# Three 256-column matmuls into one region in place of a 512- and a 256-column matmul with a join, in the weight-stationary products of a two-layer decoder trunk

## The chip, the cores and the metric

The kernel runs on one core of a Trainium2 chip. The core has a matrix engine (TensorE; PE in the profile, with its weight loads shown as a row of their own, PEld), a vector engine (VectorE, DVE), an activation engine (ScalarE, ACT), a general engine (GpSimd, POOL) and an engine that issues transfers (SyncE, SP). They run side by side and wait for one another by semaphores. Working data lies in on-chip memory of 128 partitions; the matrix engine adds its results up in a separate accumulation memory, which is divided into banks. A bank holds 512 float32 columns here.

The metric is the device time of one execution in microseconds (us), as the median of several runs.

## The reference

One sequence of 256 positions with 2048 features goes through two layers. Each layer mixes positions by attention, then applies an MLP; after each there is a residual sum and a layer norm:

```python
x = layer_norm(ALPHA * x + mixed, ln1_g[layer], ln1_b[layer])
x = layer_norm(ALPHA * x + sqrelu_mlp(x, mlp_w1[layer], mlp_w2[layer]), ...)

def sqrelu_mlp(x, w1, w2):
    hid = jax.nn.relu(jnp.einsum('bsd,df->bsf', x, w1))     # 2048 -> 8192
    return jnp.einsum('bsf,fd->bsd', hid * hid, w2)         # 8192 -> 2048
```

Layer 0 mixes with sliding-window attention (16 query heads, 2 key heads) and with three dilated window patterns of 8 heads, all from one input projection of 2048 to 5888 features. Layer 1 mixes with 16 heads of stick-breaking attention and 16 heads of latent attention, whose queries and keys come from small latent vectors. Everything is float32, and the weights are some 395 MB that are read once.

## The kernel before

**Arithmetic.** Every large product is made of three. An operand is split into a high part, rounded to the matrix engine's float32r format, and a low part, the difference. A product is hi x hi + hi x lo + lo x hi. Weights are split by the class `Stream`: units of 128 x 1024 weights come by DMA (line 95, up to 5 units ahead), are rounded on ScalarE (line 128, `w_hi`) and subtracted on VectorE (line 129, `w_lo`), up to 3 units ahead. Activations are kept feature-major in k-tiles of 128 features x 512 columns: columns 0 to 255 hold the high part of the 256 positions, columns 256 to 511 the low part (`parts`, line 300).

**Two kinds of product.** `as_` (line 348) holds activations stationary and streams weights: three matmuls per k-tile and token tile (lines 379 to 381), 512 columns wide as a rule and 256 or 288 in a few projections. It gives a token-major result. `ws` (line 312) holds weights stationary and streams activations, and gives a feature-major result. It is used for the query and key projections of layer 0 and of the stick-breaking heads, and for the first matrix of both MLPs. `uq` (line 927) does the same for the latent queries. These two are what the change touches. `ukv` (line 960) makes latent keys and values and isn't touched; its keys are weight-stationary and made by three matmuls of 256 columns each (lines 970 to 972).

**A product in `ws`.** Let the weights of 128 features and one k-tile be `wh`, `wl`, the activations `xh`, `xl`. Line 333 loads `wh` and streams both halves of the k-tile, 512 columns: the first half of the bank sums `wh` x `xh`, the second half `wh` x `xl`. Line 334 loads `wl` and streams `xh`, 256 columns, into the second half. After all 16 k-tiles the bank holds two sums, which `join` (line 341) adds: ScalarE copies the second half out of the bank, scaled (line 345, tile `xfull`), and VectorE adds the first half to it (line 346). In the MLP the ReLU is then a separate ScalarE instruction on 512 columns (line 1073), followed by the square and its split (lines 1074 to 1076). These three steps are put off to a later unit through the queue `late`.

**Loops and order.** `ws` takes the weights unit by unit. A unit of a 512-wide block holds two k-tiles of four feature tiles. For each feature tile the unit's k-tiles follow each other, so 8 products run without a break. After each unit `pump` (line 196) puts in one step of other work: a put-off step, a step of side work and a step of attention. The order of instructions on each engine is that of the program text; nothing is reordered by a scheduler.

**Banks.** There are four kinds of tiles in the accumulation memory: `acc` (4 banks), `sc` (2), `pt` (1) and `o` (1). Before, a 512-wide block of `ws` takes four banks. In the MLP every second block takes `sc`, `sc`, `pt` and `o` in place of the four `acc` (line 318), so that one block can be joined while the next is summed.

Of the kernel before, what the change touches and what calls it, by code (L numbers as in the profile page):

```python
# [67 lines left out]
class Stream:  # L68
    """Weights in the order of their use: DMA ahead, split ahead into two float32r parts.
    For the next shared units GpSimd takes a share of the second part."""  # L70
# [73 lines left out]
class LazyTiles:  # L144
    """feature-major k-tiles that are made when a product comes near them"""
# [13 lines left out]
class Job:  # L159
    """one group of attention heads: scores, then stages of the weighting, then the values"""  # L160
# [11 lines left out]
class Trunk:  # L172
# [22 lines left out]
    # ---- work beside the products: one step per unit of weights  # L195
# [17 lines left out]
    def queue(self, job, u=None):  # L213
        """all heads; pattern u only, when the patterns come one by one"""
        if u is None:
            self.todo.extend((job, h, 0) for h in range(job.n))
        else:
            self.todo.extend((job, h, u) for h in range(job.n))
# [42 lines left out]
    def flip(self, job, h, u):  # L261
        """weights of a head (and pattern) to keys-major"""
        nc = self.nc
        st = job.s[h]
        pt = self.ps.tile([P, 384], F32, name="pt")
        for b in range(3):
            nc.tensor.transpose(pt[:, b * P:(b + 1) * P], st[:, u * 384 + b * P:u * 384 + (b + 1) * P], self.ident)
        pT = self.at.tile([P, 384], F32, name="pT", bufs=self.pt_bufs)
        nc.scalar.copy(pT, pt)
        job.pt[(h, u)] = pT  # L270
        if u == job.per - 1 and (job.per > 1 or h % 2):
            self.s_live -= 1
# [30 lines left out]
    # ---- psum  # L303
# [3 lines left out]
    # ---- matrix products; xs: per k-tile (hi, lo) of [128, 256]  # L307
# [4 lines left out]
    def ws(self, xs, nkt, width, take, more=False):  # L312
        """weights stationary, feature-major result. Per 128 features one bank: the first 256 columns sum
        hi x hi, the other 256 the two cross terms; take(f, bank) is called when the sums of tile f are complete"""
        nc = self.nc
        nf = width // P
        if more:
            banks = [self.ps.tile([P, 512], F32, name=n, bufs=m) for n, m in (("sc", 2), ("sc", 2), ("pt", 1), ("o", 1))]
        else:
            banks = [self.acc() for _ in range(nf)]  # L320
        kt = 0
        while kt < nkt:
            self.near(xs, kt, 1024 // width, nkt)
            end = kt + 1024 // width >= nkt
            hi, lo, n, wd = self.w.next(ahead=self.split_ahead - end)
            assert wd == width
            self.near(xs, kt + 2, 1024 // width, nkt)
            for f in range(nf):
                for kk in range(n):
                    xh, xl, both = xs[kt + kk]  # L330
                    c = kk * width + f * P
                    first, last = kt + kk == 0, kt + kk == nkt - 1
                    nc.tensor.matmul(banks[f], hi[:, c:c + P], both, start=first, stop=False, skip_group_check=True)  # L333
                    nc.tensor.matmul(banks[f][:, S:2 * S], lo[:, c:c + P], xh, start=False, stop=last, skip_group_check=True)  # L334
                if kt + n == nkt:
                    take(f, banks[f])
            kt += n
            if kt < nkt:
                self.pump()

    def join(self, out, bank, scale=1.0):
        """both sums of a bank, scaled by a power of two"""
        nc = self.nc
        t = self.small.tile([P, S], F32, name="xfull", bufs=3)
        nc.scalar.activation(t, bank[:, S:2 * S], AF.Copy, scale=scale)  # L345
        nc.vector.scalar_tensor_tensor(out, bank[:, 0:S], scale, t, op0=ALU.mult, op1=ALU.add)

    def as_(self, xs, nkt, width, hold=0):
        """activations stationary: token-major result [128 tokens, width] for both token tiles;
        the last hold units of weights serve first the one token tile, then the other"""  # L350
# [35 lines left out]
    # ---- weights in the order in which the products below take them  # L386
# [58 lines left out]
    # ---- set-up  # L445
# [52 lines left out]
    def transposed(self, ln, z=None):  # L498
        """x (token-major) to feature-major k-tiles, split; ln=(which, layer) applies its gain and bias"""
# [28 lines left out]
    def keep_clock(self, n, t=None):  # L528
        """products that nothing takes, while the array waits, so that its clock is not halved"""
        t = self.ident if t is None else t  # L530
        o = self.ps.tile([P, 512], F32, name="pt")
        for _ in range(n):
            self.nc.tensor.matmul(o[:, 0:t.shape[1]], t[:, 0:P], t, start=True, stop=True, skip_group_check=True)

    # ---- residual sums and layer norm
# [17 lines left out]
    def rstd(self, var, n, eps, scale=1.0):  # L553
        """(var * scale + eps) ** -0.5"""
        nc = self.nc
        ve = self.small.tile([P, 2], F32, name="ve")
        nc.vector.tensor_scalar(ve[:, :n], var, scale, eps, op0=ALU.mult, op1=ALU.add)  # L557
        r = self.small.tile([P, 2], F32, name="rs")
        nc.gpsimd.tensor_tensor(r[:, :n], ve[:, :n], self.mhalf[:, :n], op=ALU.pow)  # L559
        return r  # L560

    def moments(self, last, stats):
        """the last column block into x, and per token tile the mean and 1/deviation"""
        nc = self.nc
        outs, c, first = last
        res = []
        for t in range(2):
            self.add_one(outs[t], t, c, first, stats)
            mv = self.small.tile([P, 2], F32, name="mv")
            nc.vector.bn_aggr(mv, stats[t])  # L570
            res.append((mv, self.rstd(mv[:, 1:2], 1, LN_EPS)))
            yield res[t]
# [17 lines left out]
    def x_new(self, ln, layer):  # L590
        """the residual's copy of the normed x, token-major"""
# [36 lines left out]
    def final(self, last, stats):  # L628
        """the last layer norm, token-major, to the output"""
# [33 lines left out]
    # ---- attention  # L663
    def qk(self, sc, q, k):
        """q, k: feature-major [K, 256]; sc: q-block 0 in 128 columns, q-block 1 in 256"""
# [4 lines left out]
    def softmax(self, per, scale=1.0, sink=None):  # L670
        """three stages: maximum, exponentials, division"""
# [43 lines left out]
    # ---- layer 0 mixer  # L715
    def even(self):
# [8 lines left out]
        def take(f, bank):  # L725
            self.join(kvf[:, f, :], bank)
            if f == 0:
                for kv in range(2):
                    for half in range(2):
                        eng = nc.scalar.copy if half else nc.vector.tensor_copy  # L730
                        eng(kd[half * HD:half * HD + HD, kv, :], kvf[kv * HD:kv * HD + HD, 0, :])
# [81 lines left out]
    def project(self, width, tag="qk", scale=1.0):  # L813
        """feature-major projection of x; tiles of [128, 2, 256] with two heads to a slice"""
        out = [self.tile2(tag) for _ in range(width // 256)]
        self.ws(self.xT, KT, width, lambda f, bank: self.join(out[f // 2][:, f % 2, :], bank, scale))
# [3 lines left out]
    # ---- layer 1 mixer  # L820
# [106 lines left out]
    def uq(self):  # L927
        """queries of 4 latent heads, rotated; per tile 2 heads, features in rows 0-95"""
        nc = self.nc
        banks = [self.acc() for _ in range(4)]  # L930
# [11 lines left out]
        for u in range(2):  # L942
            hi, lo, n, wd = self.w.next(ahead=self.split_ahead - u)
            for h in range(4):
                for kk in range(n):
                    xh, xl, both = self.lq[kt + kk]
                    c = (kk * 4 + h) * P
                    k = kt + kk
                    nc.tensor.matmul(banks[h], hi[:, c:c + P], both, start=k == 0, stop=False, skip_group_check=True)
                    nc.tensor.matmul(banks[h][:, S:2 * S], lo[:, c:c + P], xh, start=False, stop=k == 3, skip_group_check=True)  # L950
                if u:
                    q = qs[h // 2]
                    self.join(q[:, h % 2, :], banks[h])
                    if h % 2:
                        self.late.append(lambda q=q: rotate(q))
# [4 lines left out]
    def ukv(self):  # L960
        """keys (rows 0-63 from the latents, 64-95 the shared rotated ones) and values of 8 latent heads"""
# [91 lines left out]
    # ---- MLP  # L1053
    def mlp(self, layer):
        nc = self.nc
        st = self.new_stats()
        for q in range(4):
            hs = []
            cur = {}

            def take(f, bank):
                if f % 2 == 0:
                    cur["r"] = self.mp.tile([P, 512], F32, name="relu", bufs=3)
                r = cur["r"]
                self.join(r[:, (f % 2) * S:(f % 2) * S + S], bank)
                if f % 2 == 0:
                    return
                sq = self.mp.tile([P, 512], F32, name="sq", bufs=2)
                hh = self.mp.tile([P, 512], F32R, name="h_hi", bufs=12)
                hl = self.mp.tile([P, 512], F32R, name="h_lo", bufs=12)  # L1070

                def square():
                    nc.scalar.activation(r, r, AF.Relu)
# [8 lines left out]
            for b in range(4):  # L1082
                self.ws(self.xT, KT, 512, take, more=b % 2 == 1)
# [64 lines left out]
```

## Time and profile before

| | |
|---|---|
| time, median of 3 runs | 2272.68 us (2270.44 to 2273.03) |
| span of the profiled execution | 2269.1 us |
| TensorE matmul | 2228.8 us busy, 98%, 11633 instructions |
| TensorE weight load | 1857.5 us busy, 82%, 11633 instructions |
| VectorE | 1435.0 us busy, 63% |
| ScalarE | 1064.9 us busy, 47% |
| DMA | 399.09 MB, mean 176 GB/s |
| mean granted TensorE clock | 0.993 |

The profiled execution has its own span, 2269.1 us, from its first to its last instruction; the median of the timed runs is 3.6 us above it. Durations in the profile belong to that one execution.

Two things help to read the rows. A matmul's duration runs from its start to the end of its results, and the next one starts long before that end. So the pace of the matrix engine is not the duration of its instructions, but the distance from one start to the next. And a group's mean is of one form of instruction; the names in "out<-in" are those of the program's tiles, where `x` is a k-tile of the layer's input, `y` one of the latents or of the attention outputs, `w_hi` and `w_lo` are split weights, and `acc`, `sc`, `pt` and `o` are banks.

### The profile page before, as it was taken

The page shows a single profiled execution, that of the slowest core. Times are in us where ns is not written, and L with a number is a line of the kernel's source. Part 1 is how long each engine was busy: PE and PEld are TensorE (multiplying, and loading weights), DVE is VectorE, ACT ScalarE, POOL GpSimd, SP SyncE. Part 2 cuts the span into 40 slices and gives each one's busy share as a digit, 9 for nine tenths or more (in the row PEclk, how much of TensorE's full clock was granted, in tenths as well). Part 3 has the DMA queues.
Part 4 walks back from the last instruction along what each step waited for, and adds up shares of the span by engine and source line. Part 5 has one row for each costly group of instructions (what it writes and reads, how often), then busy time and mean ns, then how long its engine had stood idle before and what let it go on. Part 6 is the DMA issues. An engine that isn't in the chain of part 4 may idle for free. (4 is left out here: it accounts for less than half of the span.)

```text
span 2269.1 us, 30281 instructions
## 1 busy us (share of the span) xinstructions
PE 2228.8 (98%) x11633; PEld 1857.5 (82%) x11633; DVE 1435.0 (63%) x1967; ACT 1064.9 (47%) x1573; POOL 132.4 (6%) x125
## 2 busy tenths in 40 slices
PE   8999999999999999999999999999999999999997
PEld 7878787788888888888878878777888888888885
DVE  6766455785455556556567797978655655554655
ACT  4554344355345345345444575735534534443542
POOL 3000000120000000000024101003000000000001
PEclk9999999999999999999999999999999999999998
DMA  7445454465656665665658544355666566656553
GB/s 248 140 121 150 130 166 142 139 209 191 193 178 195 194 187 181 198 187 177 202 144 223 160 135 135 128 170 177 233 193 193 175 207 180 194 193 187 186 193 104
DMA packets 224322, 399.09 MB, mean 176 GB/s; under 512 B 12778, under 2 KB 56512, under 8 KB 223408
## 3 DMA queue, kind: packets, MB, share of 16 engines
q1 hardware_dynamic: 221760, 387.30, 54.6%
q0 software_dynamic: 2416, 9.84, 1.6%
q8 instruction: 91, 1.49, 0.3%
q14 instruction: 55, 0.45, 0.1%
HBM read 395.00 MB, written 2.10 MB: 175 GB/s over the span
## 5 line engine op out<-in xcount | busy, mean ns | idle before, releaser
L129 DVE TENSOR_TENSOR w_lo<-raw,w_hi 128x1024 fp32r<-128x1024 f32 (+3 forms) x748 | 879.0, 1188 | 589.9 <-ACT w_hi L128 583.0
L128 ACT CAST w_hi<-raw 128x1024 fp32r<-128x1024 f32 (+2 forms) x788 | 763.0, 986 | 777.2 <-PE acc L381 453.6
L333 PE MATMUL acc<-x,w_hi 128*128 128x512 f32 x1824 | 661.0, 405 | 12.4 <-DVE x L520 11.6
L334 PE MATMUL acc<-x,w_lo 128*128 128x256 f32 x1824 | 514.5, 282 | 0.0
L333 PEld LDWEIGHTS acc<-x,w_hi 128*128 128x128 f32 x1824 | 345.9, 190 | 106.7 <-DVE x L520 14.8
L381 PE MATMUL acc<-w_hi,h_lo 128*128 128x512 f32 x1016 | 399.3, 393 | 0.0
L380 PE MATMUL acc<-w_lo,h_hi 128*128 128x512 f32 x1016 | 398.0, 392 | 0.0
L379 PE MATMUL acc<-w_hi,h_hi 128*128 128x512 f32 x1016 | 395.6, 389 | 0.0
L334 PEld LDWEIGHTS acc<-x,w_lo 128*128 128x128 f32 x1824 | 348.0, 191 | 1.1 <-POOL w_lo L129 0.5
L380 PEld LDWEIGHTS acc<-w_lo,h_hi 128*128 128x128 f32 x1016 | 190.8, 188 | 43.2
L379 PEld LDWEIGHTS acc<-w_hi,h_hi 128*128 128x128 f32 x1016 | 190.7, 188 | 42.4
L381 PEld LDWEIGHTS acc<-w_hi,h_lo 128*128 128x128 f32 x1016 | 190.9, 188 | 39.5
L333 PE MATMUL sc<-x,w_hi 128*128 128x512 f32 x512 | 186.1, 397 | 0.0
L334 PE MATMUL sc<-x,w_lo 128*128 128x256 f32 x512 | 143.6, 281 | 0.0
L379 PE MATMUL acc<-w_hi,x 128*128 128x256 f32 (+2 forms) x400 | 137.3, 343 | 3.9 <-DVE x L519 3.8
L380 PE MATMUL acc<-w_lo,x 128*128 128x256 f32 (+2 forms) x400 | 133.4, 333 | 0.1
L381 PE MATMUL acc<-w_hi,x 128*128 128x256 f32 (+2 forms) x400 | 133.3, 333 | 0.0
L333 PEld LDWEIGHTS sc<-x,w_hi 128*128 128x128 f32 x512 | 96.1, 188 | 23.5
L559 POOL TENSOR_TENSOR rs<-ve,mhalf 128x1 f32<-128x1 f32 (+1 forms) x10 | 6.6, 659 | 1849.8 <-DVE ve L557 1843.8
L345 ACT ACTIVATE xfull<-acc 128x256 f32<-128x256 f32 x130 | 49.8, 384 | 127.0 <-PE acc L334 107.7
L334 PEld LDWEIGHTS sc<-x,w_lo 128*128 128x128 f32 x512 | 96.7, 189 | 0.0
L333 PE MATMUL o<-x,w_hi 128*128 128x512 f32 x256 | 96.0, 397 | 0.0
(194 smaller groups left out, 2376.1 us busy)
## 6 DMA issues: line engine op xcount, KB each, us to landing
raw<-in_mlp_w SPq DMA_DIRECT2D x512, 512.0 KB, 4.1
raw<-in_even_w_in SPq DMA_DIRECT2D x92, 512.0 KB, 4.0
raw<-in_odd_w_in SPq DMA_DIRECT2D x56, 512.0 KB, 4.4
raw<-in_odd_w_out SPq DMA_DIRECT2D x32, 512.0 KB, 3.7
raw<-in_even_w_out SPq DMA_DIRECT2D x24, 512.0 KB, 3.7
gb_rows<-in_ln_g POOLq DMA_DIRECT2D x3, 1024.0 KB, 6.7
gb_rows<-in_ln_b POOLq DMA_DIRECT2D x3, 1024.0 KB, 8.6
raw<-in_odd_w_uq SPq DMA_DIRECT2D x8, 384.0 KB, 3.6
```

What stands on the lines that cost most here:

```text
L128: nc.scalar.copy(h, r)
L129: (nc.gpsimd if i and perm is None else nc.vector).tensor_tensor(l, r, h.bitcast(F32), op=ALU.subtract)
L333: nc.tensor.matmul(banks[f], hi[:, c:c + P], both, start=first, stop=False, skip_group_check=True)
L334: nc.tensor.matmul(banks[f][:, S:2 * S], lo[:, c:c + P], xh, start=False, stop=last, skip_group_check=True)
L345: nc.scalar.activation(t, bank[:, S:2 * S], AF.Copy, scale=scale)
L379: nc.tensor.matmul(outs[t], xh[:, ts], hi[:, c:c + width], start=first, stop=False, skip_group_check=True)
L380: nc.tensor.matmul(outs[t], xh[:, ts], lo[:, c:c + width], start=False, stop=False, skip_group_check=True)
L381: nc.tensor.matmul(outs[t], xl[:, ts], hi[:, c:c + width], start=False, stop=last, skip_group_check=True)
L559: nc.gpsimd.tensor_tensor(r[:, :n], ve[:, :n], self.mhalf[:, :n], op=ALU.pow)
```

## The change

`ws` and `uq` no longer stream both halves of a k-tile at once. A product is three matmuls of 256 columns that add up in the same 256 columns of a bank: `wh` x `xh`, `wh` x `xl`, `wl` x `xh`, each with its own stationary operand in the program. Two feature tiles share a bank, one in each half. `join` is gone: when both feature tiles of a bank are complete, ScalarE takes the whole bank of 512 columns out at once, with the scale for projections and the ReLU for the MLP. A 512-wide block takes two `acc` banks, and the MLP no longer takes `sc`, `pt` and `o`. Comments and docstrings are removed as well.

```diff
-    def ws(self, xs, nkt, width, take, more=False):
-        nf = width // P
-        if more:
-            banks = [self.ps.tile([P, 512], F32, name=n, bufs=m) for n, m in (("sc", 2), ("sc", 2), ("pt", 1), ("o", 1))]
-        else:
-            banks = [self.acc() for _ in range(nf)]
+    def ws(self, xs, nkt, width, take):
+        banks = [self.acc() for _ in range(width // 256)]
...
-            for f in range(nf):
+            for f in range(width // P):
+                o = banks[f // 2][:, (f % 2) * S:(f % 2) * S + S]
                 for kk in range(n):
-                    xh, xl, both = xs[kt + kk]
+                    xh, xl, _ = xs[kt + kk]
                     c = kk * width + f * P
-                    first, last = kt + kk == 0, kt + kk == nkt - 1
-                    nc.tensor.matmul(banks[f], hi[:, c:c + P], both, start=first, stop=False, skip_group_check=True)
-                    nc.tensor.matmul(banks[f][:, S:2 * S], lo[:, c:c + P], xh, start=False, stop=last, skip_group_check=True)
-                if kt + n == nkt:
-                    take(f, banks[f])
+                    self.three(o, hi[:, c:c + P], lo[:, c:c + P], xh, xl, kt + kk == 0 and f % 2 == 0, kt + kk == nkt - 1)
+                if kt + n == nkt and f % 2:
+                    take(f // 2, banks[f // 2])
...
-    def join(self, out, bank, scale=1.0):
-        t = self.small.tile([P, S], F32, name="xfull", bufs=3)
-        nc.scalar.activation(t, bank[:, S:2 * S], AF.Copy, scale=scale)
-        nc.vector.scalar_tensor_tensor(out, bank[:, 0:S], scale, t, op0=ALU.mult, op1=ALU.add)
+    def three(self, o, wh, wl, xh, xl, first, last):
+        mm = self.nc.tensor.matmul
+        mm(o, wh, xh, start=first, stop=False, skip_group_check=True)
+        mm(o, wh, xl, start=False, stop=False, skip_group_check=True)
+        mm(o, wl, xh, start=False, stop=last, skip_group_check=True)
...
-        self.ws(self.xT, KT, width, lambda f, bank: self.join(out[f // 2][:, f % 2, :], bank, scale))
+        self.ws(self.xT, KT, width, lambda p, bank: self.nc.scalar.activation(
+            out[p].rearrange("p a s -> p (a s)"), bank, AF.Copy, scale=scale))
...
-                self.join(r[:, (f % 2) * S:(f % 2) * S + S], bank)
-                if f % 2 == 0:
-                    return
+            def take(p, bank):
+                r = self.mp.tile([P, 512], F32, name="relu", bufs=3)
+                nc.scalar.activation(r, bank, AF.Relu)
...
                 def square():
-                    nc.scalar.activation(r, r, AF.Relu)
                     nc.scalar.activation(hh, r, AF.Square)
...
-                self.ws(self.xT, KT, 512, take, more=b % 2 == 1)
+                self.ws(self.xT, KT, 512, take)
```

`uq` and the take-out of the shared keys in layer 0 are changed in the same way.

More of the change, by code (lines that the diff above doesn't have):

```diff
@@ L310, in near @@
             xs.need(min(kt + n - 1, nkt - 1))
-    def ws(self, xs, nkt, width, take, more=False):
-        nc = self.nc
-        nf = width // P
-        if more:
-            banks = [self.ps.tile([P, 512], F32, name=n, bufs=m) for n, m in (("sc", 2), ("sc", 2), ("pt", 1), ("o", 1))]
-        else:
-            banks = [self.acc() for _ in range(nf)]
+    def ws(self, xs, nkt, width, take):
+        banks = [self.acc() for _ in range(width // 256)]
         kt = 0
@@ L339, in ws @@
                 self.pump()
-    def join(self, out, bank, scale=1.0):
-        nc = self.nc
-        t = self.small.tile([P, S], F32, name="xfull", bufs=3)
-        nc.scalar.activation(t, bank[:, S:2 * S], AF.Copy, scale=scale)
-        nc.vector.scalar_tensor_tensor(out, bank[:, 0:S], scale, t, op0=ALU.mult, op1=ALU.add)
+    def three(self, o, wh, wl, xh, xl, first, last):
[3 more added lines that the diff above has]
+        mm(o, wl, xh, start=False, stop=last, skip_group_check=True)
     def as_(self, xs, nkt, width, hold=0):
@@ L723, in even @@
         vf = kvf[:, 1, :]
[L725 to L731, printed above, removed]
+        def take(p, bank):
+            nc.scalar.copy(kvf.rearrange("p a s -> p (a s)"), bank)
+            for kv in range(2):
+                for half in range(2):
+                    eng = nc.scalar.copy if half else nc.vector.tensor_copy
+                    eng(kd[half * HD:half * HD + HD, kv, :], kvf[kv * HD:kv * HD + HD, 0, :])
         self.ws(self.xT, KT, 256, take)
@@ L929, in uq @@
         nc = self.nc
-        banks = [self.acc() for _ in range(4)]
+        banks = [self.acc() for _ in range(2)]
         qs = [self.tile2("d") for _ in range(2)]
@@ L944, in uq @@
             for h in range(4):
+                o = banks[h // 2][:, (h % 2) * S:(h % 2) * S + S]
                 for kk in range(n):
-                    xh, xl, both = self.lq[kt + kk]
+                    xh, xl, _ = self.lq[kt + kk]
                     c = (kk * 4 + h) * P
[L948 to L951, printed above, removed]
+                    self.three(o, hi[:, c:c + P], lo[:, c:c + P], xh, xl, kt + kk == 0 and h % 2 == 0, kt + kk == 3)
+                if u and h % 2:
                     q = qs[h // 2]
-                    self.join(q[:, h % 2, :], banks[h])
-                    if h % 2:
-                        self.late.append(lambda q=q: rotate(q))
+                    nc.scalar.copy(q.rearrange("p a s -> p (a s)"), banks[h // 2])
+                    self.late.append(lambda q=q: rotate(q))
             kt += n
@@ L1058, in mlp, with take @@
             hs = []
-            cur = {}
-            def take(f, bank):
-                if f % 2 == 0:
-                    cur["r"] = self.mp.tile([P, 512], F32, name="relu", bufs=3)
-                r = cur["r"]
-                self.join(r[:, (f % 2) * S:(f % 2) * S + S], bank)
-                if f % 2 == 0:
-                    return
+            def take(p, bank):
+                r = self.mp.tile([P, 512], F32, name="relu", bufs=3)
                 sq = self.mp.tile([P, 512], F32, name="sq", bufs=2)
```

## The prediction, made before the result

> **What bounds the kernel now.** I read the page first, then the waits of the matrix engine, its groups by shape, and its timeline.
>
> ```profile
> span 2269.1 us, 30281 instructions
> PE 2228.8 (98%) x11633; PEld 1857.5 (82%) x11633; DVE 1435.0 (63%) x1967; ACT 1064.9 (47%) x1573; POOL 132.4 (6%) x125
> PEclk9999999999999999999999999999999999999998
> ```
>
> The matrix engine is busy for 98% of the span at a granted clock of 0.9 or more of full speed in all but the last slice. Busy is not the same as "at its best", because records of pipelined matmuls overlap; so I ask next what it waits for, and then how far apart its matmuls start.
>
> ```profile
> PE acc L333 <- DVE x L520: 11.6, 9, 3.6
> PE acc L379 <- DVE x L519: 3.8, 1, 3.8
> PE sc L667 <- DVE S L1026: 2.4, 5, 1.1
> PE acc L333 <- ACT w_hi L128: 0.4, 2, 0.2
> ```
>
> The columns are the total in us, the number of times and the longest. The large waits are those for the split x tiles after a layer norm (lines 519 and 520), which the change doesn't touch. Split weights cost 0.4 us in all, and no line says that a matmul waits for a bank that a join has still to empty. So the time is the sum of start-to-start distances on the matrix engine, and the change must be priced there.
>
> ```profile
> L333 PE MATMUL acc<-x,w_hi 128*128 128x512 f32 x1824 | 661.0, 405 | 12.4 <-DVE x L520 11.6 <-ACT w_hi L128 0.4
> L333 PE MATMUL sc<-x,w_hi 128*128 128x512 f32 x512 | 186.1, 397 | 0.0
> L333 PE MATMUL o<-x,w_hi 128*128 128x512 f32 x256 | 96.0, 397 | 0.0
> L333 PE MATMUL pt<-x,w_hi 128*128 128x512 f32 x256 | 95.9, 397 | 0.0
> L949 PE MATMUL acc<-y,w_hi 128*128 128x512 f32 x64 | 23.4, 405 | 0.0
> L379 PE MATMUL acc<-w_hi,x 128*128 128x256 f32 x192 | 56.4, 294 | 0.0
> L970 PE MATMUL acc<-y,w_hi 128*128 128x256 f32 x16 | 4.8, 302 | 0.0
> ```
>
> The first five rows give the number of products that are changed: 1824 + 512 + 256 + 256 + 64 = 2912 (a product is one block of 128x128 weights against one k-tile). The last two rows are places where the kernel before already does three 256-column matmuls per product.
>
> **The change on the matrix engine.** Now a product is one matmul of 512 columns and one of 256, each with its own weight load. Afterwards it is three of 256, each with its own load: the streamed columns stay at 768, one load and one start are added. The pace of the pair, from the timeline (columns: start, duration, engine, line), in the MLP of layer 0 and then in that of layer 1:
>
> ```profile
> 879.61 0.40 PE L333 MATMUL sc<-x,w_hi 128*128 128x512 f32 x1
> 879.85 0.28 PE L334 MATMUL sc<-x,w_lo 128*128 128x256 f32 x1
> ...
> 895.87 0.39 PE L379 MATMUL acc<-w_hi,h_hi 128*128 128x512 f32 x1
> ```
>
> ```profile
> 1609.78 0.40 PE L333 MATMUL acc<-x,w_hi 128*128 128x512 f32 x1
> ...
> 1628.16 0.39 PE L333 MATMUL pt<-x,w_hi 128*128 128x512 f32 x1
> ```
>
> The first stretch holds 46 pairs without a gap: (895.87 - 879.61) / 46 = 0.3535 us. The second holds 53: (1628.16 - 1609.78) / 53 = 0.3468 us. The same instructions thus run at two paces. I take 0.352 for the mean, about three parts of the slow one to one of the fast one; that weight is my choice. Both exceed what the streamed columns ask for, so loads are already not free.
>
> Three matmuls of 256 columns with three loads, first from line 379 (x stationary, weights streamed), a run of 24 without a gap:
>
> ```profile
> 205.03 0.28 PE L379 MATMUL acc<-w_hi,x 128*128 128x256 f32 x1
> 205.15 0.28 PE L380 MATMUL acc<-w_lo,x 128*128 128x256 f32 x1
> ...
> 207.78 0.28 PE L381 MATMUL acc<-w_hi,x 128*128 128x256 f32 x1
> ```
>
> 23 distances in 2.75 us are 0.1196 us each, or 0.3587 for three. Second, from lines 970 to 972, which have the operands in the changed kernel's own roles (weights stationary, activations streamed, the first load repeated), two stretches of them:
>
> ```profile
> 1326.54 0.28 PE L971 MATMUL acc<-y,w_hi 128*128 128x256 f32 x1
> ...
> 1327.67 0.28 PE L972 MATMUL acc<-y,w_lo 128*128 128x256 f32 x1
> ...
> 1330.21 0.28 PE L971 MATMUL acc<-y,w_hi 128*128 128x256 f32 x1
> ...
> 1331.51 0.40 PE L976 MATMUL acc<-w_hi,y 128*128 128x512 f32 x1
> ```
>
> The first has 10 distances in 1.13 us, 0.113 each (0.339 for three); the second 11 in 1.30 us, 0.1182 each (0.3545). So the bounds for a triple are 0.339 and 0.3587, and against 0.352 the change costs between -0.013 and +0.0067 us per product, that is -38 to +20 us over 2912. That the low end is a gain is no slip: it needs only that the added load hides wholly under 256 columns.
>
> How close that is, the weight loads show:
>
> ```profile
> 205.04 0.19 PEld L380 LDWEIGHTS acc<-w_lo,x 128*128 128x128 f32 x1
> 205.16 0.19 PEld L381 LDWEIGHTS acc<-w_hi,x 128*128 128x128 f32 x1
> ```
>
> A load starts just after the matmul before it has started (205.03, 205.15), and the next matmul starts when it is through, 0.11 to 0.12 us later. Under 512 columns a load has twice that time; under 256 the load and the stream are about equally long, and any slip of either shows. The change turns the one comfortable position of a product into two tight ones.
>
> I take 0.1191 per matmul: two parts of 0.1196 to one of 0.1182, so 0.3574 for three. I lean to line 379 because it works on the same x tiles as nearly all changed products and has 192 of each matmul where line 970 has 16, and because its run is twice as long: the changed MLP blocks run 192 matmuls without a break. The roles of the operands speak for line 970; its slower stretch is what I let count. Cost: (0.3574 - 0.352) x 2912 = **+15.7 us**.
>
> Here the Trainium skill speaks both for and against. "TensorE: Matmul & The Clock Gate" says under "Step-by-step: what each phase is for" that the array reads streamed operands and weights through two independent ports, so that a load takes nothing from a running matmul; under "Back-to-back issue gap" it prices an isolated warm matmul at columns / 2.4 + 2.5 ns. By this, an estimate, a product goes from 325.0 to 327.5 ns, +7.3 us in all, since only one start is added. The trace disagrees with the price: 0.1196 us stands where that formula gives 0.109.
>
> **Joins and evacuations.** A join is one activation on ScalarE and one add on VectorE.
>
> ```profile
> L345 ACT ACTIVATE xfull<-acc 128x256 f32<-128x256 f32 x130 | 49.8, 384 | 127.0 <-PE acc L334 107.7 <-issue 9.2 <-PE acc L950 8.5
> L346 DVE SCALAR_TENSOR_TENSOR relu<-acc,xfull 128x256 f32<-128x256 f32 x64 | 27.2, 425 | 40.1 <-ACT xfull L345 40.1
> L1073 ACT ACTIVATE relu<-relu 128x512 f32<-128x512 f32 x64 | 40.0, 625 | 0.0
> ```
>
> There is one join per 128 features. Removed are 2912 / 16 = 182 minus the 64 latent products' share of 4, so 178 from x, and 64 / 4 = 16 from the latents: 194. That is 194 x 0.384 = 74 us on ScalarE and 194 x 0.425 = 82 us on VectorE; the ReLU of the MLP moves into the evacuation, which saves its separate 40 us. Added are 97 evacuations of 512 columns on ScalarE; with no row for one from a bank, I price them between two of 0.384 and the 0.625 of line 1073, and take 0.65: 63 us. VectorE so loses 82 us and ScalarE 51 us of work, at 63% and 47% busy. Nearly all of it lies under matmuls. What can surface is a part of the 2.4 us for attention scores and of the small waits beside it; I take **-2 us**, between 0 and -5. The x-tile waits stay: the first matmul of a product now needs only the high part, but the second needs the low part right behind it.
>
> Nothing moves on the DMA queues. The sums take two banks where they took four, and the MLP no longer borrows the banks of scores, transposes and attention outputs; with no wait on banks in the table this is worth 0. Evacuating two tiles at once delays the first of the pair by at most its two matmul groups of the last unit, about 0.7 us; a block's next user comes a whole unit later, 8 x 0.352 = 2.8 us, which covers it. Without that cover it would cost under 0.7 us in each of some 50 blocks, 35 us at the very most.
>
> **Sum.** 2269.1 + 15.7 - 2 = 2282.8 us for a profiled span; the median of the runs shown, 2272.68, is 3.6 above that of before, so 2286 us.
>
> **The rivals.**
> - *The added load hides* (faster). Place: the three matmuls of each product. It decides at 0.352 / 3 = 0.1173 us per matmul; below that the change gains. At the 0.113 of the first stretch of line 971 the time is 2272.7 - 38 - 2 = 2233; at a pace between, 0.1155, it is 2272.7 - 16 - 2 = 2255. For: the roles of the operands, and a fast and a slow stretch there. Against: the run of line 379 doesn't reach it.
> - *Splitting costs almost nothing* (no change). The 1330 stretch's 0.1182 held throughout gives (0.3545 - 0.352) x 2912 = +7.3, less up to 5 from the side work: 2275 to 2280; at 0.1175 it would be 2272.7 + 1.5 - 2 = 2272. For: it is the middle of all the rows. Against: both places show paces away from it. The skill's price above lands here too.
> - *The second load of the same weights is skipped*, so that no load is added. Two of three loads then hold the product at the 0.3468 of the fast pair or below: 2272.7 - 15 - 2 = 2256. Against: lines 379 and 380 use one stationary tile in turn, and the loads at 205.04 and 205.16 still follow each matmul.
> - *The joins were in the way*: all waits of that kind gone, 2268. Against: the table of waits.
>
> **How the numbers follow.** I give the forecast of a slower kernel 0.52, no change 0.16, the hidden load 0.28, the skipped load 0.02, the joins 0.02. About 0.2% (4.5 us) can be told from no change: below 2268 faster, above 2277 slower. The upper part of the second case goes to slower: faster 0.31, same 0.15, slower 0.54. The likeliest case alone runs from 2277 to 2300: its top is 0.120 per matmul, +23 us, and a mean pair a little faster than my 0.352. The whole range must reach into the hidden load: 2242 leaves out about 1 in 10 below, 2300 somewhat less above.
>
> **What would show it.** The count of loads and matmuls must rise by 2912 each. In the MLP, where nothing interrupts, the distance of three matmuls of a product is the test: 0.357 to 0.360 bears me out, 0.352 is no change, 0.340 to 0.347 is the hidden load. Lines 345 and 346 must be gone and VectorE's busy time lower by some 80 us with the table of matrix-engine waits hardly altered. I am wrong if the pace in runs of 192 matmuls differs from that in runs of 24 or 12, in either direction, since nothing before shows a run that long; or if the x-tile waits grow.

## The result and the profile after

The changed kernel takes 2289.25 us (2287.38 to 2291.5, 4 runs), the kernel before 2271.56 us (2270.37 to 2273.03, 4 runs, those shown above and one more): a ratio of 1.0083, 95% interval 1.007 to 1.0095. It is slower by 17.7 us, where some 14 us were forecast. The profiled execution grew from a span of 2269.1 to 2287.5 us, by 18.4.

From the page of the changed kernel, the span and the engines; then the three groups of a product of x (line 338 is `wh` x `xh`, line 339 `wh` x `xl`, line 340 `wl` x `xh`; lines 513 and 514 are lines 519 and 520 of before):

```profile
span 2287.5 us, 35748 instructions
PE 2248.2 (98%) x14545; PEld 2014.5 (88%) x14545; DVE 1354.4 (59%) x1773; ACT 1009.0 (44%) x1412; POOL 131.0 (6%) x125
...
L338 PE MATMUL acc<-x,w_hi 128*128 128x256 f32 x2848 | 815.3, 286 | 7.6 <-DVE x L513 7.6
L339 PE MATMUL acc<-x,w_hi 128*128 128x256 f32 x2848 | 810.8, 285 | 3.0 <-DVE x L514 2.2
L340 PE MATMUL acc<-x,w_lo 128*128 128x256 f32 x2848 | 808.4, 284 | 0.9 <-POOL w_lo L129 0.9
```

Matmuls and loads rose by 14545 - 11633 = 2912 each, one per product: no load of repeated weights is skipped. VectorE's busy time fell by 80.6 us and ScalarE's by 55.9, and the span grew all the same. So neither of these engines set the end. The timeline of the changed kernel, in the MLP of layer 0 (the first and the last start of line 338 in a stretch without gaps, 50 products apart):

```profile
859.90 0.28 PE L338 MATMUL acc<-x,w_hi 128*128 128x256 f32 x1
...
877.90 0.28 PE L338 MATMUL acc<-x,w_hi 128*128 128x256 f32 x1
```

18.00 / 50 = 0.360 us per product, where the pair took 0.3535. The same three matmuls on the latents, a few us into a run, 10 products apart:

```profile
1267.98 0.28 PE L338 MATMUL acc<-y,w_hi 128*128 128x256 f32 x1
...
1271.39 0.28 PE L338 MATMUL acc<-y,w_hi 128*128 128x256 f32 x1
```

These take 3.41 / 10 = 0.341 us, faster than the pair. One kernel thus shows both of the main cases of the prediction at once: the load costs with x, and hides with the latents. Why is what the experiments had to settle.

The waits of the matrix engine in the changed kernel (total us, times, longest):

```profile
PE acc L338 <- DVE x L513: 7.6, 3, 3.2
PE acc L373 <- DVE x L513: 3.8, 1, 3.8
PE sc L500 <- DVE x_res L578: 3.3, 8, 0.5
PE acc L339 <- DVE x L514: 2.2, 3, 1.1
...
PE sc L661 <- DVE S L1018: 1.6, 2, 1.0
```

The wait for the low part of x, 11.6 us before, is now one for the high part and a short one for the low part, 9.8 together. The wait for a bank of attention scores, 2.4 us before, is 1.6. New is the 0.9 us in the row of line 340 above, for low weights that GpSimd makes (line 129 gives a part of some units to it).

### The profile page after: what moved, and what is told of

Read it like the earlier page. It is cut to its first block, busy times and chain, and to the rows that moved or that the text cites. A ratio compares the mean times of both kernels' runs of the same rounds, so it can differ in the third digit from the quotient of the medians.

```text
span 2287.5 us, 35748 instructions
## 1 busy us (share of the span) xinstructions
PE 2248.2 (98%) x14545; PEld 2014.5 (88%) x14545; DVE 1354.4 (59%) x1773; ACT 1009.0 (44%) x1412; POOL 131.0 (6%) x125
## 4 chain that ended last, share of the span: by engine, by line
PE 64%; issue 30%; DVE 5%; ACT 1%; DMA 0%; POOL 0%; SPq 0%; DVEq 0%; ACTq 0%; POOLq 0%
PE acc L338 10%; PE acc L339 10%; PE acc L340 10%; PE acc L373 9%; PE acc L374 9%; PE acc L375 9%; PE pt L267 1%; DVE w_lo L129 1%; PE o L286 1%; PE sc L662 1%; PE sc L661 1%; DVE x L513 1%; DVE x_res L578 1%; DVE x L514 1%; DVE sb_a L1032 1%
## 5 line engine op out<-in xcount | busy, mean ns | idle before, releaser
L338 PE MATMUL acc<-x,w_hi 128*128 128x256 f32 x2848 | 815.3, 286 | 7.6 <-DVE x L513 7.6
L339 PE MATMUL acc<-x,w_hi 128*128 128x256 f32 x2848 | 810.8, 285 | 3.0 <-DVE x L514 2.2
L340 PE MATMUL acc<-x,w_lo 128*128 128x256 f32 x2848 | 808.4, 284 | 0.9 <-POOL w_lo L129 0.9
L338 PEld LDWEIGHTS acc<-x,w_hi 128*128 128x128 f32 x2848 | 545.0, 191 | 16.0 <-DVE x L513 8.2
L339 PEld LDWEIGHTS acc<-x,w_hi 128*128 128x128 f32 x2848 | 545.0, 191 | 8.1 <-DVE x L514 7.4
L340 PEld LDWEIGHTS acc<-x,w_lo 128*128 128x128 f32 x2848 | 545.1, 191 | 1.2 <-POOL w_lo L129 1.1
L1057 ACT ACTIVATE relu<-acc 128x512 f32<-128x512 f32 x64 | 38.2, 598 | 135.7 <-PE acc L340 135.7
L1061 DVE TENSOR_TENSOR sq<-relu 128x512 f32<-128x512 f32 x64 | 47.1, 736 | 81.3 <-ACT relu L1057 81.3
L373 PEld LDWEIGHTS acc<-w_hi,x 128*128 128x128 f32 x400 | 76.2, 190 | 19.6 <-issue 7.5
L375 PEld LDWEIGHTS acc<-w_hi,x 128*128 128x128 f32 x400 | 76.3, 191 | 7.9 <-DVE x L514 0.6
```

What stands on the lines that cost most here:

```text
L338: mm(o, wh, xh, start=first, stop=False, skip_group_check=True)
L339: mm(o, wh, xl, start=False, stop=False, skip_group_check=True)
L340: mm(o, wl, xh, start=False, stop=last, skip_group_check=True)
L373: nc.tensor.matmul(outs[t], xh[:, ts], hi[:, c:c + width], start=first, stop=False, skip_group_check=True)
L375: nc.tensor.matmul(outs[t], xl[:, ts], hi[:, c:c + width], start=False, stop=last, skip_group_check=True)
L1057: nc.scalar.activation(r, bank, AF.Relu)
```

## The experiments

All were timed beside the kernel before, and each ratio is to it. The layout of the on-chip memory comes from the kernels themselves: per partition, the split weights begin at byte 42240 and their tiles are 4096 bytes long, the x tiles begin at 91392 and are 2048 long. Both positions are 256 modulo 512. The latents begin at 960 modulo 1024, which is 704 bytes off that grid.

**The shape alone: `split_keep_join`.** From the kernel before:

```diff
-  nc.tensor.matmul(banks[f], hi[:, c:c + P], both, start=first, stop=False, skip_group_check=True)
+  nc.tensor.matmul(banks[f][:, 0:S], hi[:, c:c + P], xh, start=first, stop=False, skip_group_check=True)
+  nc.tensor.matmul(banks[f][:, S:2 * S], hi[:, c:c + P], xl, start=False, stop=False, skip_group_check=True)
```

> The kernel before with one edit: the 512-column matmul of a product becomes two of 256 columns with a load each; the halves of the bank, the joins and the use of the banks stay as before. Theory 'load' (a third load and start under short matmuls is what costs): the MLP's products go at 0.360 us as in the changed kernel, and the time is the changed kernel's plus the side work that the joins bring, 2289 to 2293 us. Rival 'region' (three sums in a row into the same 256 columns hold each other up): two of the three matmuls now go to different halves, so products go at 0.347 to 0.353 us and the time is 2270 to 2278 us.

Its timeline in the MLP of layer 0, first and last start of a product's first matmul, 50 products apart:

```profile
859.74 0.28 PE L333 MATMUL acc<-x,w_hi 128*128 128x256 f32 x1
...
877.74 0.28 PE L333 MATMUL acc<-x,w_hi 128*128 128x256 f32 x1
```

0.360 us per product, 2287.8 us, ratio 1.0084 (1.0068 to 1.0101). The time is just under the 2289 to 2293 us expected, beside a kernel before at 2269.28 us. The whole loss is there with joins, separate halves and banks as before. Summing three times into one region is not the cause, and taking the joins away is worth nothing that can be measured: the change without them has the ratio 1.0083.

**The order of the loads: `order_hi_lo_hi`.** From the changed kernel:

```diff
   mm(o, wh, xh, start=first, stop=False, skip_group_check=True)
-  mm(o, wh, xl, start=False, stop=False, skip_group_check=True)
-  mm(o, wl, xh, start=False, stop=last, skip_group_check=True)
+  mm(o, wl, xh, start=False, stop=False, skip_group_check=True)
+  mm(o, wh, xl, start=False, stop=last, skip_group_check=True)
```

> The changed kernel with the second and third matmul of a product exchanged: high weights, low weights, high weights again, so that no two loads in a row read the same weights. Theory 'address' and theory 'load': no change, 0.360 us per product, 2287 to 2292 us. Rival 'same weights' (a load of weights that are being used collides with itself): 0.347 to 0.353 us per product, 2251 to 2270 us.

```profile
859.87 0.28 PE L338 MATMUL acc<-x,w_hi 128*128 128x256 f32 x1
...
877.87 0.28 PE L338 MATMUL acc<-x,w_hi 128*128 128x256 f32 x1
```

The same view gives 18.00 / 50 = 0.360 us again; 2286.95 us, ratio 1.0081 (1.0066 to 1.0096). Loading the same weights twice in a row does no harm of its own.

**Where x lies: `after_x704` and `before_x704`.** Small tiles that lay behind the x tiles are laid ahead of them. The instructions and their order stay:

```diff
+        self.pre = pool("pre", 5)
         self.res = pool("res", 1)
...
-        return [self.small.tile([P, 4, 6], F32, name=f"bn{t}", bufs=2) for t in range(2)]
+        return [self.pre.tile([P, 4, 6], F32, name=f"bn{t}", bufs=2) for t in range(2)]
...
-        mv = self.small.tile([P, 2], F32, name="mv")
+        mv = self.pre.tile([P, 2], F32, name="mv")
```

The tile `ve` is moved in the same way; the four come to 704 bytes. In the kernel before the edit is the same.

> The changed kernel with one edit: four small tiles (704 bytes per partition) are laid ahead of the x tiles instead of behind them, so that the x tiles lie at byte 960 within a stretch of 1024, as the latents of layer 1 do, and no longer at 256 as the split weights do. Same instructions in the same order. Theory 'address' (the loss per load hangs on where the streamed operand lies against the stationary one; the latents' products of the changed kernel went at 0.340 us with these same three matmuls): products of x at 0.340 us, 2848 x 0.0195 = 56 us less, 2228 to 2240 us. Rival 'load' (every load under 256 columns costs a fixed time, and the latents are fast only because their runs are short): 0.360 us, 2287 to 2291 us.

The timeline of the shifted changed kernel in the MLP of layer 0 (line 339 is now `wh` x `xh`), a stretch of 52 products, and an earlier one of 33:

```profile
850.04 0.28 PE L339 MATMUL acc<-x,w_hi 128*128 128x256 f32 x1
...
867.72 0.28 PE L339 MATMUL acc<-x,w_hi 128*128 128x256 f32 x1
```

```profile
520.06 0.28 PE L339 MATMUL acc<-x,w_hi 128*128 128x256 f32 x1
...
531.72 0.28 PE L339 MATMUL acc<-x,w_hi 128*128 128x256 f32 x1
```

17.68 / 52 = 0.340 us, and 11.66 / 33 = 0.3533 us: two paces, the fast one in most of the run. The time is 2239.32 us, ratio 0.9869 (0.9853 to 0.9885). Nothing but the place of tiles moved the same instructions from 0.8% slower than the kernel before to 1.3% faster. "Every load costs a fixed time" falls here, and so does the thought that the latents were fast because their runs are short.

> The kernel before with the same shift of the x tiles by 704 bytes. Theory 'address': the pairs go at one pace, as the pairs of the latents do in the kernel before (0.235 + 0.118 = 0.353 us), with no stretch at 0.347: 2272 to 2278 us. Rival 'phase' (the two paces of the pair come from how a run of matmuls happens to start): both paces are still there, 2269 to 2274 us.

The pairs of the kernel before, with the same shift, 51 products apart:

```profile
859.64 0.40 PE L334 MATMUL acc<-x,w_hi 128*128 128x512 f32 x1
...
877.66 0.40 PE L334 MATMUL pt<-x,w_hi 128*128 128x512 f32 x1
```

0.3533 us; 2274.51 us, ratio 1.0021 (1.0012 to 1.0031). The stretches at 0.347 of layer 1 are gone from the trace, as expected. So the pairs depend on the place too, but here the shift costs.

**Which distance counts: `after_x512`, `after_x192`, `after_x1280`.** The same edit with other small tiles.

> The changed kernel with the x tiles 512 bytes further on (three small tiles laid ahead of them instead of behind). A weight block of 128 float32 is 512 bytes, and every stationary block and every streamed half starts at a multiple of 512 from its tile's start; so if the distance of the two streams counts within a block only (theory 'address modulo 512'), nothing changes: 0.360 us per product, 2285 to 2291 us. Rival 'any shift' (what counts is a longer pattern, or that the tiles moved at all): 0.340 to 0.354 us, 2230 to 2275 us.

```profile
860.07 0.28 PE L339 MATMUL acc<-x,w_hi 128*128 128x256 f32 x1
...
877.71 0.28 PE L339 MATMUL acc<-x,w_hi 128*128 128x256 f32 x1
```

17.64 / 49 = 0.360 us, 2288.71 us, ratio 1.0083 (1.0065 to 1.0101): as without a shift.

> The changed kernel with the x tiles 192 bytes further on, which is 704 modulo 512. Theory 'address modulo 512': as with 704, products at 0.340 us with some stretches at 0.353, 2236 to 2243 us. Rival 'any shift': something else than with 704.

```profile
849.98 0.28 PE L339 MATMUL acc<-x,w_hi 128*128 128x256 f32 x1
...
868.00 0.28 PE L339 MATMUL acc<-x,w_hi 128*128 128x256 f32 x1
```

18.02 / 53 = 0.340 us, 2240.32 us, ratio 0.987 (0.9851 to 0.9888): as with 704.

> The changed kernel with the x tiles 1280 bytes further on, that is 256 modulo 512, half a weight block from the weights' own position. Theory 'address modulo 512' says only that the pace may be another one; if the loss comes from the two streams meeting at the same place, half a block away is as far as they can be: 0.340 us throughout without stretches at 0.353, 2230 to 2238 us. If 192 is a lucky place: 0.347 to 0.360 us, 2250 to 2290 us.

```profile
859.88 0.28 PE L339 MATMUL acc<-x,w_hi 128*128 128x256 f32 x1
...
877.88 0.28 PE L339 MATMUL acc<-x,w_hi 128*128 128x256 f32 x1
```

18.00 / 50 = 0.360 us, 2288.7 us, ratio 1.0083 (1.0063 to 1.0103). My picture of two streams that meet in one place and are best off half a block apart was wrong: 1280 is as bad as 0. The three together fit a distance that counts modulo 256; of places 256 bytes apart, only 0 and 256 were tried.

**A finer distance: `after_x320` and `after_x160`.**

> The changed kernel with the x tiles 320 bytes further on. So far shifts of 0, 512 and 1280 bytes gave 0.360 us per product, 192 and 704 gave 0.340 with stretches at 0.353; both groups agree modulo 128 (0 and 64) as well as modulo 256 (0 and 192). 320 is 64 modulo 128 and 64 modulo 256. Theory 'modulo 128': as with 192, 0.340 us with stretches at 0.353, 2236 to 2246 us. Theory 'modulo 256': a pace of its own; 0.347 to 0.360 us and 2255 to 2290 us if only 192 is lucky.

First the weight-stationary products, 51 apart; then, in layer 0, the activation-stationary triples of 256 columns (line 374, which is line 379 of before), 6 triples apart:

```profile
859.94 0.28 PE L339 MATMUL acc<-x,w_hi 128*128 128x256 f32 x1
...
877.96 0.28 PE L339 MATMUL acc<-x,w_hi 128*128 128x256 f32 x1
```

```profile
204.54 0.28 PE L374 MATMUL acc<-w_hi,x 128*128 128x256 f32 x1
...
206.58 0.28 PE L374 MATMUL acc<-w_hi,x 128*128 128x256 f32 x1
```

18.02 / 51 = 0.3533 us; 2270.04 us, ratio 0.9998 (0.9989 to 1.0008). So it isn't modulo 128: 64 and 192 differ. The second view fits with a sign. There the weights stream and x is stationary, so a shift of x by 64 puts the streamed operand at -64, which is 192 modulo 256, and the triple goes at 2.04 / 6 = 0.340 us, where it took 0.3587 without a shift. The same triples with the shift of 704 must then be at -192, which is 64 modulo 256. Six of them:

```profile
205.26 0.28 PE L374 MATMUL acc<-w_hi,x 128*128 128x256 f32 x1
...
207.38 0.28 PE L374 MATMUL acc<-w_hi,x 128*128 128x256 f32 x1
```

2.12 / 6 = 0.3533 us (a few other runs of them go at 0.340), as the weight-stationary products at 64. So in both roles the pace follows the position of the streamed operand minus that of the stationary one. That is the simplest reading of both signs; no run moved both operands by the same amount to prove it.

> The changed kernel with the x tiles 160 bytes further on, which is 32 modulo 128. If the pace depends on the distance of the two streams in steps finer than 64 bytes, it is a third pace between 0.340 and 0.360 us, 2237 to 2289 us; if only the 64-byte row counts in which a word lies, 160 lies in the row that begins 128 on, an even one, and the pace is that of no shift: 0.360 us, 2285 to 2291 us.

```profile
859.95 0.28 PE L339 MATMUL acc<-x,w_hi 128*128 128x256 f32 x1
...
877.75 0.28 PE L339 MATMUL acc<-x,w_hi 128*128 128x256 f32 x1
```

17.80 / 50 = 0.356 us, 2280.43 us, ratio 1.0043 (1.0029 to 1.0057): a pace of its own. There is a second one, in layer 1, 31 products apart, (1283.83 - 1272.92) / 31 = 0.352 us:

```profile
1272.92 0.28 PE L339 MATMUL acc<-x,w_hi 128*128 128x256 f32 x1
...
1283.83 0.28 PE L339 MATMUL acc<-x,w_hi 128*128 128x256 f32 x1
```

That steps finer than 64 bytes count does not follow. The expectation took the row that begins at 128 to act like the one at 0, because both are even; no run tried 128, and after the run with 320 nothing says that the two are alike. In the other role the same run puts the operands at -160, that is 96, and six triples of line 374 take 0.360 us:

```profile
252.56 0.28 PE L374 MATMUL acc<-w_hi,x 128*128 128x256 f32 x1
...
254.72 0.28 PE L374 MATMUL acc<-w_hi,x 128*128 128x256 f32 x1
```

**The hidden tiles too: `after_x704_h64`.** 64 bytes are laid ahead of the MLP's tiles, beside the shift of x by 704.

> The changed kernel with the x tiles shifted by 704 bytes and, in the MLP, 64 bytes laid ahead of the hidden tiles, so that these lie like the weights (256 modulo 512). In the kernel before, the token-major triples of 512 columns go at 0.680 us where the stationary tile lies like the weights (x) and at 0.687 where it doesn't (h, y). Theory 'address': the second MLP products, 1024 triples, go from 0.687 to 0.680 us, 7 us less than with the first shift alone: 2230 to 2236 us. Rival: the 0.007 us come from the kind of tile and not from its place: 2237 to 2242 us.

The activation-stationary triples of 512 columns in the MLP (line 374), 36 triples apart, first with the shift of x alone, then with both; third, the weight-stationary products with both, 45 apart:

```profile
894.69 0.39 PE L374 MATMUL acc<-w_hi,h_hi 128*128 128x512 f32 x1
...
919.41 0.39 PE L374 MATMUL acc<-w_hi,h_hi 128*128 128x512 f32 x1
```

```profile
894.91 0.39 PE L374 MATMUL acc<-w_hi,h_hi 128*128 128x512 f32 x1
...
919.39 0.39 PE L374 MATMUL acc<-w_hi,h_hi 128*128 128x512 f32 x1
```

```profile
859.95 0.28 PE L339 MATMUL acc<-x,w_hi 128*128 128x256 f32 x1
...
875.85 0.28 PE L339 MATMUL acc<-x,w_hi 128*128 128x256 f32 x1
```

The triples do go from 24.72 / 36 = 0.6867 to 24.48 / 36 = 0.680 us, as expected. Yet the time is 2252.97 us, ratio 0.9927 (0.9915 to 0.9939), 13 us above that of the first shift: the weight-stationary products, whose own tiles didn't move, now go at 15.90 / 45 = 0.3533 in the place where they went at 0.340. At this distance two paces are possible. That the matmuls ahead decide which one a run falls into is what the timelines suggest; it wasn't tested by itself. Each MLP runs in four rounds of first and second products. With the shift of x alone, the first round of layer 0 is the only one of the eight whose weight-stationary products go at 0.3533 nearly throughout (the stretch from 520.06 above). Its activation-stationary triples, right behind, are also the only ones that don't go at 0.687, though their place is the same; 36 triples apart, 25.20 / 36 = 0.700 us:

```profile
540.48 0.40 PE L374 MATMUL acc<-w_hi,h_hi 128*128 128x512 f32 x1
...
565.68 0.40 PE L374 MATMUL acc<-w_hi,h_hi 128*128 128x512 f32 x1
```

**Is it the place alone? `before_x320` and `split_x704`.**

> The kernel before with the x tiles 320 bytes further on, 64 modulo 256. With no shift its pairs go at 0.347 or 0.353 us, with 704 (192 modulo 256) at 0.353 throughout. Theory 'address': one pace again, and it may be another one. If no placement brings a pair below 0.347, the three short matmuls with the right placement (0.340) are the better form: 2262 to 2280 us. If the pair reaches 0.340 here, the placement alone is the gain and the form doesn't matter: 2236 to 2245 us.

```profile
859.62 0.40 PE L334 MATMUL acc<-x,w_hi 128*128 128x512 f32 x1
...
878.00 0.39 PE L334 MATMUL sc<-x,w_hi 128*128 128x512 f32 x1
```

18.38 / 52 = 0.3535 us, in a few stretches 0.349; 2271.04 us, ratio 1.0005 (0.9996 to 1.0015).

> The kernel before with the 512-column matmul split into two of 256 (joins and banks as before) and the x tiles shifted by 704 bytes: the changed kernel at its good placement, but with the joins. If the joins and the banks are worth nothing, as the two kernels without a shift say (ratios 1.0083 and 1.0084 to the kernel before), it takes what the shifted changed kernel takes, a ratio of 0.985 to 0.989 and 2236 to 2244 us. If they matter once the matrix engine is faster, it is 5 us or more above: 2245 to 2260 us.

```profile
849.97 0.28 PE L334 MATMUL acc<-x,w_hi 128*128 128x256 f32 x1
...
867.99 0.28 PE L334 MATMUL sc<-x,w_hi 128*128 128x256 f32 x1
```

18.02 / 53 = 0.340 us, 2240.27 us, ratio 0.9872 (0.9853 to 0.9891). With joins and borrowed banks the good placement takes what it takes without them (0.9869). So the gain needs the short matmuls and the place together: the pair came to no less than 0.347 at the three places tried, the triple to 0.340.

## Why the prediction was right

**The bound.** Right. All runs follow the pace of the products; in the changed kernel 80 us of VectorE's and 56 us of ScalarE's work are gone and are worth nothing measurable, as `split_keep_join` and `split_x704` show from the other side.

**The product's cost.** Right in sign, undersized. The sum took 0.352 us for the pair and 0.3574 for the triple, +15.7 us. The 0.352, a weight of choice, was right: over the 2669 distances under 0.42 us between one pair of x and the next, the trace of before has a mean of 0.3518. The triple was sized too low. Its measured 0.360 lies above even the upper bound of 0.3587, and yet it stands in the very run of line 379 from which that bound was read. The last four triples of that run:

```profile
206.10 0.28 PE L379 MATMUL acc<-w_hi,x 128*128 128x256 f32 x1
...
207.54 0.28 PE L379 MATMUL acc<-w_hi,x 128*128 128x256 f32 x1
```

They take 1.44 / 4 = 0.360 us each, the three ahead of them 1.07 / 3 = 0.357. The average over the run took its start in with its steady part. With 0.360 the term is (0.360 - 0.352) x 2912 = +23.3 us.

One reading behind the cost is off. The prediction says that the next matmul starts when its load is through. In the rows that it shows, the load of line 380 starts at 205.04 and lasts 0.19 us, to 205.23, and its matmul starts at 205.15. So these rows don't show that a load and 256 streamed columns are equally long, and why a third load costs at this place stays open.

**The choice between the rows.** The slower row was the right one to lean on, and of the reasons given one holds: it works on the same x tiles. The other, that its runs are longer, is refuted: runs of 192 matmuls in the MLP go at 0.340 once x is moved. The split by roles of the operands was a wrong lead as well; the latents were fast for where they lie. Their two stretches, 0.339 and 0.3545, are close to the two paces that a distance of 192 showed with x, 0.340 and 0.3533. So the 0.3574, a mean of line 379 and the slower of these, mixed two places.

**What was luck.** The prediction has no place in it, and the direction hung on the place. With the x tiles 704 bytes further on, the kernel before takes 2274.51 us and the changed kernel 2239.32, 1.5% less: there the same change is a gain. "Slower" came true because the weights and the x tiles happen to lie alike modulo 256, and the row of line 379, which has the same tiles, carried that in unnamed.

**The signs of being wrong.** The x-tile waits did not grow. The other sign, another pace in runs of 192 matmuls than in runs of 24 or 12, is half met: 0.360 is the pace of the run of 24 once it is steady, and not that of the runs of 12. But the place makes the difference and not the length.

**What gave back.** The -2 us for joins weren't there: of the waits, 0.8 us for scores went and 0.9 for weights came. But the total was 18.4 us in the profile and not 23, so some 5 us came back elsewhere. Two parts can be named: the waits for split x tiles, said to stay, went from 11.6 to 9.8 us, since the first matmul of a product now asks for the high part alone; and the 64 latent products at 0.341 cost 64 x (0.360 - 0.341) = 1.2 us less than the term has. The remaining 2 us weren't traced.

**Evacuations.** Priced at 0.65 us each; measured:

```profile
L1057 ACT ACTIVATE relu<-acc 128x512 f32<-128x512 f32 x64 | 38.2, 598 | 135.7 <-PE acc L340 135.7
```

0.598, off the path. No matmul waits for a bank that an evacuation has to empty, as said; the one wait on a bank in the table is that for scores.

**The rivals.** "The added load hides" was the right second: it is what happens on the latents, and on x with another placement, at 2239 us, some 6 above the 2233 that the fast stretch of line 971 gave. Its deciding point, 0.1173 us per matmul, holds: 0.1133 gains, 0.1178 (the 0.3533 of the 320-byte shift) comes out even, 0.120 loses. The Trainium skill ("TensorE: Matmul & The Clock Gate", "Step-by-step: what each phase is for") gives the array two independent read ports, so that a load takes nothing from a running matmul. The traces agree only at some places: at distance 0, splitting a matmul, which adds a load and a start, took a product from 0.347 or 0.3535 to 0.360 us, and at 192 the same three matmuls took 0.340.

## What to carry to other kernels

Price a change of matmul shapes by start-to-start distances from rows with the same tiles, and treat a spread between such rows as a question, not as noise: here 0.339 against 0.359 us for the same three matmuls was worth more than the whole change. In long runs of short matmuls with a load each, try the relative place of the two operands before deciding on a form: moving 704 bytes of small tiles turned the slower of the two forms into the faster one, 2239.32 us against 2269.28 for the kernel before beside it. Try it for each form by itself, since a place that suits one form can cost another time, as the next section shows. Freeing work on engines that aren't the bound, and banks that nothing waits for, buys nothing.

## What was not expected of the hardware

The start-to-start distance of float32r matmuls with a load each depended here on the byte positions of their operands, and all readings fit the position of the streamed operand minus that of the stationary one. For three matmuls of 256 columns, by this distance modulo 256:

| distance | us per product |
|---|---|
| 0 (shifts of 0, 512, 1280) | 0.360 |
| 64 (shift of 320) | 0.353 |
| 96 (shift of 160, activations stationary) | 0.360 |
| 160 (shift of 160) | 0.356, in stretches 0.352 |
| 192 (shifts of 192, 704) | 0.340, in stretches 0.353 |

For three of 512 columns with weights streamed, the hidden tiles took 0.680 us at distance 0 and 0.687, in one block 0.700, at 64. The x tiles in the same role show that the best place for short matmuls is not the best for long ones. At distance 192 (shift of 320), 11 triples of 512 columns took 7.70 / 11 = 0.700 us:

```profile
404.54 0.39 PE L374 MATMUL acc<-w_hi,x 128*128 128x512 f32 x1
...
412.24 0.39 PE L374 MATMUL acc<-w_hi,x 128*128 128x512 f32 x1
```

Without a shift they take 0.680 in the changed kernel, and with the shift of 704, at 64, 0.687. For a pair of 512 and 256, the paces are 0.347 or 0.353 at 0, 0.353 with a few stretches at 0.349 at 64, and 0.353 at 192. One and the same code can run at two paces at one distance, steadily for whole blocks. What in the memory or the array causes it, no run here shows; that modulo 256 is the true period rests on six shifts besides none, and other distances than those of the table weren't tried.
